# First feed-forward product of a Griffin-style block: 20 of 22 pairs by seven block products

## The chip, the cores and the metric

The kernel runs on one core of one Trainium2 chip. The metric is the device time of one execution in microseconds (us); the kernel before takes 917.13 us, the median of three runs (917.04 to 917.58).

The core has five engines that run side by side and wait for each other through semaphores: PE multiplies matrices, DVE (VectorE) and ACT (ScalarE) work on whole tiles, POOL (GpSimd) does slower tile work and can issue transfers, SP only issues transfers. Weight loads into PE have a row of their own, PEld. The profile's times count from the start of the span, which is the stretch from the first to the last instruction.

## What is computed

One layer of a streaming encoder over 512 tokens of 1024 features, all in float32: three parallel mixers, cross-attention into 256 memory tokens, and a gated feed-forward block. The change touches the last part only:

```python
h = rms_norm(x, g_ffn_pre[l])
f_gate, f_up = jnp.split(h @ w_ffn_in[l], 2, axis=-1)      # 1024 -> 2 x 2816
x = x + rms_norm((jax.nn.silu(f_gate) * f_up) @ w_ffn_out[l], g_ffn_post[l])
```

`w_ffn_in` is 1024 x 5632 and `w_ffn_out` 2816 x 1024.

## The kernel before

**Three matmuls for one.** Each float32 operand is kept as a high part, rounded to the matmul's own format by a cast on ACT, and a low part, the difference, made by a subtraction on DVE or POOL. A product is the sum of three matmuls, high by high, high by low and low by high (`mm3`, L89 to L92). So every weight tile costs a load on SP's queue (L173), a cast on ACT (L191) and a subtraction, either one on DVE (L195) or two halves on POOL (L198, L199). The list `low` says which engine is next; `low_on("g")` sends all to POOL, `low_on("v")` all to DVE, `low_on("vg")` alternates.

**First product, pair by pair.** 128 gate columns of `w_ffn_in` and the 128 up columns that belong to them are a pair; there are 22 pairs. A unit is one of the two: `unit` runs 8 chunks of 128 features, each `mm3` over all 512 tokens, 24 matmuls of 512 columns. A pair is two units, 48 matmuls. `hh` and `hl` hold the normed tokens turned to features, 8 chunks by 512 tokens. `swiglu` takes the two sums from PSUM: tanh on ACT (L1126), two DVE steps (L1127, L1128), and then the split of the result into high and low (L1129 on ACT, L1130 on DVE).

**The first two pairs** (`NFIRST` = 4 units) start before all tokens are normed: `unit_piece` does them in two halves of 256 columns, tokens 0 to 255 first. In between, token blocks 2 and 3 are normed and turned (`R[2].turn()`, `R[3].turn()`): `turn_pe` transposes on PE (L294), `turn_out` casts to `hh` on ACT (L302) and subtracts to `hl` on DVE (L303).

**Second product.** `project` runs over the 22 chunks of 128 hidden columns; each needs one tile of `w_ffn_out` and 24 matmuls of 512 columns over 4 token blocks.

**What sets the order.** Storage is taken from pools of slots, first given back, first taken: 6 raw weight tiles (RAW), 4 split ones (WH, WL), 8 PSUM banks (PS), 10 tiles of 128 x 512 (T2), 13 of 128 x 2048 by then (K8). The code is written in one sequence; a scheduler then sets the order on each engine, and each engine works strictly in it. `prefetch` splits weights two units ahead.

## Time and profile before

| | |
|---|---|
| median of three runs | 917.13 us |
| the profiled execution | 914.67 us |
| its span, first to last instruction | 912.9 us |
| granted clock of PE, mean | 0.997 of full speed |
| first two pairs, start of their matmuls | 537.67 us |
| the other 20 pairs | 563.3 to 783.7 us |
| second product and the end | 783.7 to 912.9 us |

The stages are read from the timeline of PE: the matmuls of the first product carry the names `hh,k` and `hh,x` with 256 columns (first two pairs) and `hh,wh` with 512 (the other pairs); those of the second have `wh` as the moving operand and `k` or `x` as the stationary one. A row of the timeline gives start, duration, engine, line and tiles; matmuls overlap, so the time that one takes out of PE is the distance between starts, not the duration. The profiled execution is 2.46 us shorter than the median; sums are made against the profiled one.

### The profile page before, as it was taken

How to read it: one execution, taken by the hardware profiler on the slowest of the kernel's cores; microseconds unless marked ns; L12 is line 12 of the kernel's file. 1: busy time of each engine (PE TensorE's matmuls, PEld its weight loads, DVE VectorE, ACT ScalarE, POOL GpSimd, SP SyncE). 2: the span in 40 equal slices, each digit the busy share in tenths (PEclk: the TensorE clock that was granted, in tenths of full speed). 3: DMA queues.
4: the chain of work that ended last, by engine and by line, in shares of the span. 5: the costliest groups of instructions: out<-in, count | busy, mean ns of one | idle time of the engine just before them, and what ended most of it. 6: DMA issues, size and time to landing. Idle time of an engine off the chain costs nothing.

```text
span 912.9 us, 11068 instructions
## 1 busy us (share of the span) xinstructions
PE 885.9 (97%) x4179; PEld 730.5 (80%) x4179; DVE 499.8 (55%) x889; ACT 344.3 (38%) x575; POOL 231.2 (25%) x203
## 2 busy tenths in 40 slices
PE   7999999999999999999989989999999999999997
PEld 6788888888788788888868779888888888888885
DVE  5769989946773745311876783433334443222225
ACT  4465553225654544322655452222223222211121
POOL 2223464644444322344561460000000000000000
PEclk9999999999999999999999999999999999999999
DMA  8953237333332245333454230333333332333102
GB/s 245 242 128 93 70 93 184 93 94 91 104 81 77 75 150 185 96 107 97 117 161 115 70 116 1 93 93 98 104 97 93 93 93 92 96 99 104 48 1 93
DMA packets 122801, 95.42 MB, mean 105 GB/s; under 512 B 5568, under 2 KB 111612, under 8 KB 122748
## 3 DMA queue, kind: packets, MB, share of 16 engines
q1 hardware_dynamic: 120172, 90.52, 34.5%
q10 hardware_dynamic: 2576, 4.19, 1.3%
q8 instruction: 33, 0.54, 0.2%
q14 instruction: 20, 0.16, 0.1%
HBM read 86.83 MB, written 2.10 MB: 97 GB/s over the span
## 4 chain that ended last, share of the span: by engine, by line
PE 88%; DVE 5%; issue 2%; ACT 2%; POOL 1%; DMA 1%; ACTq 0%; DVEq 0%; SPq 0%; POOLq 0%
PE ps L91 28%; PE ps L90 28%; PE ps L92 28%; PE ps L450 1%; PE ps L775 1%; PE ps L760 1%; PE ps L294 1%; DVE wl L195 1%; DVE hl L303 1%; DVE k L932 1%; POOL wl L199 1%; POOL y L274 1%; DVE c L278 0%; DVE k L393 0%; DMA k<-t 0%
## 5 line engine op out<-in xcount | busy, mean ns | idle before, releaser
L191 ACT CAST wh<-raw 128x1024 fp32r<-128x1024 f32 (+1 forms) x144 | 150.5, 1047 | 388.9 <-issue 154.3
L91 PE MATMUL ps<-hl,wh 128*128 128x512 f32 (+2 forms) x736 | 285.5, 388 | 3.7 <-DVE hl L303 3.7
L90 PE MATMUL ps<-hh,wh 128*128 128x512 f32 (+2 forms) x736 | 285.9, 389 | 0.3 <-ACT hh L302 0.3
L92 PE MATMUL ps<-hh,wl 128*128 128x512 f32 (+2 forms) x736 | 285.4, 388 | 0.0
L195 DVE TENSOR_TENSOR wl<-raw,wh 128x1024 fp32r<-128x1024 f32 x79 | 98.2, 1243 | 163.0 <-ACT wh L191 163.0
L91 PEld LDWEIGHTS ps<-hl,wh 128*128 128x128 f32 (+1 forms) x736 | 137.6, 187 | 34.0 <-DVE hl L303 4.6
L90 PEld LDWEIGHTS ps<-hh,wh 128*128 128x128 f32 (+1 forms) x736 | 137.4, 187 | 30.0 <-ACT hh L302 0.5
L92 PEld LDWEIGHTS ps<-hh,wl 128*128 128x128 f32 (+1 forms) x736 | 137.5, 187 | 29.7
L198 POOL TENSOR_TENSOR wl<-raw,wh 128x512 fp32r<-128x512 f32 (+1 forms) x65 | 88.9, 1368 | 199.4 <-ACT wh L191 178.2
L274 POOL TENSOR_TENSOR y<-u,half 128x1 f32<-128x1 f32 x26 | 15.1, 587 | 415.5 <-DVE u L271 384.6
L199 POOL TENSOR_TENSOR wl<-raw,wh 128x512 fp32r<-128x512 f32 (+1 forms) x65 | 91.8, 1412 | 0.0
L90 PE MATMUL ps<-wh,k 128*128 128x512 f32 x192 | 75.8, 395 | 0.0
L91 PE MATMUL ps<-wl,k 128*128 128x512 f32 x192 | 75.5, 393 | 0.0
L92 PE MATMUL ps<-wh,k 128*128 128x512 f32 x176 | 69.7, 396 | 0.0
L90 PE MATMUL ps<-k,wh 128*128 128x512 f32 (+1 forms) x128 | 47.2, 369 | 0.0
L1128 DVE TENSOR_TENSOR t<-t,ps 128x512 f32<-128x512 f32 x22 | 15.1, 688 | 58.5 <-PE ps L92 58.5
L92 PE MATMUL ps<-k,wl 128*128 128x512 f32 (+1 forms) x128 | 46.9, 366 | 0.0
L92 PE MATMUL ps<-wh,x 128*128 128x512 f32 x112 | 44.2, 395 | 0.0
L91 PEld LDWEIGHTS ps<-wl,k 128*128 128x128 f32 x192 | 36.1, 188 | 8.1
L90 PEld LDWEIGHTS ps<-wh,k 128*128 128x128 f32 x192 | 36.0, 188 | 8.2
L92 PEld LDWEIGHTS ps<-wh,k 128*128 128x128 f32 x176 | 33.4, 190 | 8.1 <-DVE k L393 0.2
L90 PE MATMUL ps<-wh,x 128*128 128x512 f32 x96 | 38.8, 404 | 0.0
(210 smaller groups left out, 1173.7 us busy)
## 6 DMA issues: line engine op xcount, KB each, us to landing
raw<-in_w_in SPq DMA_DIRECT2D x45, 512.0 KB, 4.0
raw<-in_w_ffn_in SPq DMA_DIRECT2D x44, 512.0 KB, 3.8
raw<-in_w_ffn_out SPq DMA_DIRECT2D x22, 512.0 KB, 3.5
raw<-in_w_branch SPq DMA_DIRECT2D x12, 512.0 KB, 3.4
k<-t SPq DMA_DIRECT2D x32, 128.0 KB, 2.4
raw<-in_w_out SPq DMA_DIRECT2D x8, 512.0 KB, 3.6
raw<-in_w_mem_kv SPq DMA_DIRECT2D x8, 512.0 KB, 3.6
k<-in_x ACTq DMA_DIRECT2D x2, 1024.0 KB, 8.9
```

The source lines that it names most:

```text
L90: T.matmul(o, lh, rh, start=start, stop=False, skip_group_check=True)
L91: T.matmul(o, lh, rl, start=False, stop=False, skip_group_check=True)
L92: T.matmul(o, ll, rh, start=False, stop=stop, skip_group_check=True)
L191: copy = A.copy(h, src)
L195: V.tensor_sub(l, src, f32(h))
L198: G.tensor_sub(l[:, :c], src[:, :c], f32(h[:, :c]))
L199: G.tensor_sub(l[:, c:], src[:, c:], f32(h[:, c:]))
L274: G.tensor_tensor(y, u, half, op=OP.pow)
L294: T.transpose(ps[:, k], src[:, (4 * q + k) * P:(4 * q + k + 1) * P], ident)
L303: V.tensor_sub(hl[:, 4 * q:4 * q + 4, dst], ps, f32(h))
L450: T.matmul(ps[:, :n], q[j][:, hp, r], k[i][:, :n], start=i == 0, stop=i == 1, skip_group_check=True)
L1128: V.tensor_mul(th, th, pu)
```

## The change

A pair is seen as a 2 x 2 matrix of blocks: gate and up columns by the first and the last 512 features (a11, a12 for gate, a21, a22 for up), and the tokens as 2 x 2 too (features 0 to 511 and 512 to 1023, by tokens 0 to 255, LO, and 256 to 511, HI: b11, b21, b12, b22). The 2 x 2 product of blocks is formed from seven block products in place of eight (Winograd's form of Strassen's scheme, with its signs placed otherwise). A block product is 4 chunks of `mm3` over 256 columns, 12 matmuls; a pair has 84 matmuls of 256 columns. The first two pairs and the second product keep their matmuls.

- **Weight sums** s1 to s4 per pair, each 128 x 512: s1 and s2 by additions on DVE, s3 and s4 by transfers that POOL issues and that add to their target (`accum_op`). `first`, `second` and `third` split two blocks each (cast 128 x 1024 on ACT, subtraction on DVE), `fourth` splits s4.
- **Token sums** t1 to t4, once: taken from the turned blocks while they are in PSUM. Blocks 0 and 1 are also copied whole to SBUF (`whole`), blocks 2 and 3 give differences (`turn_tokens`), and `token_sums` splits the four sums.
- **`swiglu`** writes the result unsplit; the split (`halve`) moves to the second product, up to 4 chunks ahead. `before` and `behind` are the hooks in `project`.
- **Order**: the sums and splits of the next pair are written between the products of this one; products 3 and 4 of a pair stand between the first products of the next one. The splits of the first four units are written ahead of the output projection of the memory attention (`prefetch(4 + NFIRST)`), and alternate between DVE and POOL; the two `low_on` settings in the first product are gone, so the tiles of `w_ffn_out` alternate too.

```diff
-        while (state["split"] < min(len(specs), want) and raws
+        while (state["split"] < min(state["last"], want) and raws
...
+    prefetch(4 + NFIRST)
...
     def after_o(t, pss):
         R.append(Residual(t, pss, g_post, g_next))
-        if t == 0:
-            low_on("g")
-            prefetch(4 + NFIRST)
...
+    whole = K8.take([P, 2, 4, 256])
+
+    def turn_tokens(t, pss):
+        if t < 2:
+            for q in range(2):
+                A.copy(whole[:, q, :, t * P:(t + 1) * P], pss[q])
+            PS.give(*pss)
+            return None
+        c12, d1, d3 = (T2.take([P, 4, P]) for _ in range(3))
+        A.copy(c12, pss[0])
+        V.tensor_sub(d1, whole[:, 0, :, (t - 2) * P:(t - 1) * P], pss[0])
+        V.tensor_sub(d3, pss[1], c12)
+        PS.give(*pss)
+        return c12, d1, d3
...
     def swiglu(m, pg, pu):
-        act_tiles(m)
         th = T2.take([P, S])
         A.activation(th, pg, AF.Tanh, scale=0.5)
         V.scalar_tensor_tensor(th, th, 1.0, pg, op0=OP.add, op1=OP.mult)
-        V.tensor_mul(th, th, pu)
-        A.activation(ah[m], th, AF.Copy, scale=0.5)
-        V.scalar_tensor_tensor(al[m], th, 0.5, f32(ah[m]), op0=OP.mult, op1=OP.subtract)
+        V.scalar_tensor_tensor(act_tile(m), th, 0.5, pu, op0=OP.mult, op1=OP.mult)
...
+    def token_sums(t, c12, d1, d3):
+        r = slice((t - 2) * P, (t - 1) * P)
+        d2, d4 = T2.take([P, 4, P]), T2.take([P, 4, P])
+        V.scalar_tensor_tensor(d2, d3, -1.0, whole[:, 0, :, r], op0=OP.mult, op1=OP.subtract)
+        V.scalar_tensor_tensor(d4, d2, -1.0, whole[:, 1, :, r], op0=OP.mult, op1=OP.subtract)
+        for name, src in (("t2", d2), ("t1", d1), ("t3", d3), ("t4", d4)):
...
+            h, l = (x[:, :, r] for x in tokens[name][:2])
+            tc.keep_in_program_order(A.copy(h, src))
+            tc.keep_in_program_order(V.tensor_sub(l, src, f32(h)))
...
+        def two(self, names, src, pin):
+            h, l = WH.take([P, KD, P], F32R), WL.take([P, KD, P], F32R)
+            both = self.split(names, src, h, l, pin)
...
+        def sums(self, pin=False):
+            s2, s1 = self.s[:, 0:4], self.s[:, 4:8]
+            ins = [V.tensor_add(s1, self.u_[:, 0:4], self.u_[:, 4:8]),
+                   V.tensor_add(s2, s1, self.g_[:, 0:4])]
...
+            G.dma_start(self.u_[:, 0:4], self.g_[:, 0:4], accum_op=OP.add)
+        def first(self, pin=False):
+            self.two(["a11", "a12"], self.g_, pin)
+        def second(self, pin=False):
+            self.two(["s2", "s1"], self.s, pin)
+        def third(self, pin=False):
+            self.two(["s3", "a22"], self.u_, pin)
+            RAW.give(self.u_)
+        def fourth(self, pin=False):
+            s4 = self.g_[:, 4:8]
+            G.dma_start(s4, self.s[:, 0:4], accum_op=OP.add)
+            h, l = T2.take([P, 4, P], F32R), T2.take([P, 4, P], F32R)
+            self.split([], s4, h, l, pin)
+            self.u["s4"] = (h, l, None)
+            RAW.give(self.g_)
+            load_ahead()
+        def product(self, o, a_, b, start, stop):
+            (h, l, both), (bh, bl) = self.u.pop(a_), tokens[b][:2]
+            for k in range(4):
+                mm3(o, h[:, k], l[:, k], bh[:, k], bl[:, k], start and k == 0, stop and k == 3)
...
+        def p1(self):
+            self.x, self.y = PS.take([P, 2, TH]), PS.take([P, S])
+            self.v, self.up = T2.take([P, S]), T2.take([P, S])
+            self.product(self.x[:, 0], "a11", "b11", True, False)
+            A.copy(self.v[:, LO], self.x[:, 0])
...
+        def p5(self):
+            self.product(self.y[:, HI], "s1", "t1", True, False)
+            V.tensor_add(self.up[:, HI], self.v[:, HI], self.y[:, HI])
+        def p7(self):
+            self.product(self.x[:, 1], "s3", "t3", True, False)
+            V.tensor_add(self.up[:, HI], self.up[:, HI], self.x[:, 1])
+        def p3(self):
+            self.product(self.y[:, HI], "s4", "b22", False, True)
+        def p4(self):
+            self.product(self.x[:, 1], "a22", "t4", False, True)
+            V.tensor_add(self.up[:, LO], self.v[:, HI], self.x[:, 1])
+            V.tensor_add(self.v, self.v, self.y)
...
-    for m in range(NFIRST // 2, NFF):
-        if m == NFIRST // 2 + 1:
-            low_on("v")
-        w0, w1 = take_w(), take_w()
-        pg, pu = PS.take([P, S]), PS.take([P, S])
-        unit(pg, w0)
-        unit(pu, w1)
-        swiglu(m, pg, pu)
+    while cur is not None:
+        nxt = Pair(cur.m + 1) if cur.m + 1 < NFF else None
+        if nxt is None:
+            state["last"] = len(specs)
+        cur.p1()
+        if nxt:
+            nxt.sums()
+        if old:
+            old.p3()
+        cur.p2()
+        if old:
+            old.p4()
+        if nxt:
+            nxt.first()
+        cur.p6()
+        if nxt:
+            nxt.second()
+        cur.p5()
+        cur.p7()
+        if nxt:
+            nxt.third()
+            nxt.fourth()
+        old, cur = cur, nxt
```

The scheduler's order moves at two places that matter here. The first is DVE in the pairs. Before, five rows make one pair: `wl` is the low part of a unit's weights, `ps` the two sums of a pair, `k` its result.

```order
L195 TENSOR_TENSOR wl_87_5220<-raw_91_4680,wh_87_5219 128x1024
L1127 SCALAR_TENSOR_TENSOR t_4_173_5213<-t_4_173_5213,ps_251_5163 128x512
L1128 TENSOR_TENSOR t_4_173_5213<-t_4_173_5213,ps_252_5164 128x512
L195 TENSOR_TENSOR wl_88_5226<-raw_92_4686,wh_88_5225 128x1024
L1130 SCALAR_TENSOR_TENSOR k_4_65_5134<-t_4_173_5213,k_8_64_5133 128x512
```

Now, the twelve rows of one pair's time. The matmuls of pair 6 (`ps_259`, `ps_260`) run meanwhile; `wl_98` to `wl_100` and `t_5_208` are the splits of pair 7 (`first`, `second`, `third`, `fourth`); L1206 and L1207 are the sums s1 of pair 9 and s2 of pair 9; L1259 and L1263 follow products 5 and 7 of pair 6, L1270 and L1271 product 4 of pair 5, L1275 and L1276 its result.

```order
L1192 TENSOR_TENSOR wl_98_5721<-raw_97_5409,wh_98_5720 128x1024
L1270 TENSOR_TENSOR t_8_200_5538<-t_1_199_5537,ps_257_5535 128x256
L1192 TENSOR_TENSOR wl_99_5738<-k_9_69_5067,wh_99_5737 128x1024
L1271 TENSOR_TENSOR t_1_199_5537<-t_1_199_5537,ps_258_5536 128x512
L1206 TENSOR_TENSOR k_9_69_5067<-raw_102_5656 128x512
L1259 TENSOR_TENSOR t_4_205_5661<-t_9_204_5660,ps_260_5659 128x256
L1192 TENSOR_TENSOR wl_100_5768<-raw_98_5411,wh_100_5767 128x1024
L1275 SCALAR_TENSOR_TENSOR t_6_206_5716<-t_6_206_5716,t_1_199_5537 128x512
L1263 TENSOR_TENSOR t_4_205_5661<-t_4_205_5661,ps_259_5658 128x256
L1276 SCALAR_TENSOR_TENSOR x_1_71_5596<-t_6_206_5716,t_8_200_5538 128x512
L1192 TENSOR_TENSOR t_5_208_5773<-raw_97_5409,t_3_207_5772 128x512
L1207 TENSOR_TENSOR k_9_69_5067<-k_9_69_5067,raw_101_5654 128x512
```

Five rows for a pair have become twelve, and two of the twelve (L1259, L1263) stand between a block product and a later product into the same part of a PSUM bank.

The second place is POOL where the memory attention ends and the first product begins. Before (`raw_87` to `raw_90` are the weights of pairs 2 and 3; L274 is a power of one column in the norms):

```order
L198 TENSOR_TENSOR k_9_60_4682<-raw_86_4439,k_9_60_4682 128x512
L199 TENSOR_TENSOR k_9_60_4682<-raw_86_4439,k_9_60_4682 128x512
L274 TENSOR_TENSOR y<-u,half 128x1 x5
L198 TENSOR_TENSOR wl_83_4893<-raw_87_4582,wh_83_4892 128x512
L199 TENSOR_TENSOR wl_83_4893<-raw_87_4582,wh_83_4892 128x512
L198 TENSOR_TENSOR wl_84_4900<-raw_88_4589,wh_84_4899 128x512
L199 TENSOR_TENSOR wl_84_4900<-raw_88_4589,wh_84_4899 128x512
```

Now:

```order
L198 TENSOR_TENSOR k_4_58_4605<-raw_86_4439,k_4_58_4605 128x512
L199 TENSOR_TENSOR k_4_58_4605<-raw_86_4439,k_4_58_4605 128x512
L274 TENSOR_TENSOR y<-u,half 128x1 x8
L1211 DMA raw_88_4587<-raw_87_4580 128x512
L1225 DMA raw_87_4580<-k_9_69_5067 128x512
L1211 DMA raw_90_4598<-raw_89_4592 128x512
L1211 DMA raw_92_4609<-raw_91_4603 128x512
```

The eight half-subtractions of pairs 2 and 3 (four of them stand in what is shown) are gone from POOL, and it goes on with the adding transfers, two for each pair.

More of the change, by code (lines that the diff above doesn't have):

```diff
@@ L166, in hybrid_block_kernel @@
     raws, ready = collections.deque(), collections.deque()
-    state = {"load": 0, "split": 0, "taken": 0, "low": 0}
+    state = {"load": 0, "split": 0, "taken": 0, "low": 0, "last": first_ffn + NFIRST}
     def load_ahead(n=None):
@@ L887, in project @@
             give_w(w)
+            if behind:
+                behind(k)
+        if before:
+            before(nk)
         ws = [take_w() for _ in range(hold)]
@@ L1139, in hybrid_block_kernel @@
             if c == 0 and i == 2:
-                R[2].turn()
                 R[3].norm()
+                ds = R[2].turn(turn_tokens)
         if c == 0:
-            R[3].turn()
+            token_sums(3, *R[3].turn(turn_tokens))
+            token_sums(2, *ds)
+            K8.give(whole)
+            tokens.update(b11=quad(0, 0), b21=quad(1, 0), b22=quad(1, 1))
+            scratch = K8.take([P, 2, KD, P])
+            cur = Pair(NFIRST // 2)
+            for f in (cur.first, cur.sums, cur.second, cur.third, cur.fourth):
+                f()
     give_w(*ws)
-    low_on("g")
     for m in range(NFIRST // 2):
```

104 lines of the change are left out of this document (86 added, 18 removed).

## The prediction

> **What bounds the kernel now.** I read the page first, then the table by stage, then the timeline of PE for what one matmul takes out of it.
>
> The page's busy times, and its chain that ended last by engine:
>
> ```profile
> span 912.9 us, 11068 instructions
> PE 885.9 (97%) x4179; PEld 730.5 (80%) x4179; DVE 499.8 (55%) x889; ACT 344.3 (38%) x575; POOL 231.2 (25%) x203
> ...
> PE 88%; DVE 5%; issue 2%; ACT 2%; POOL 1%; DMA 1%; ACTq 0%; DVEq 0%; SPq 0%; POOLq 0%
> ```
>
> PE is busy nearly throughout, and the chain is mostly PE. What the change is worth must be read in the stages it touches. The table by stage gives for each stretch its length, then busy time and count of PE, PEld, DVE, ACT and POOL, the granted clock, the share of DMA and GB/s:
>
> ```profile
> 563.30:783.70 220.40, 220.40 (x960) 179.92 (x959) 85.63 (x99) 61.59 (x79) 0.00 (x0) 1.00 0.32 93
> 783.70:912.90 129.20, 122.41 (x529) 98.96 (x528) 37.91 (x53) 25.96 (x36) 2.19 (x4) 0.99 0.21 70
> ```
>
> The first row is the 20 pairs: 960 matmuls, PE busy for the whole of 220.40 us at full clock, so 220.40 / 960 = 0.2296 us for one of 512 columns, and 48 x 0.2296 = **11.02 us for a pair**. DVE has 85.63 / 20 = 4.28 us of work in it, ACT 3.08, POOL none. Only fewer PE columns make this stage shorter.
>
> **The block products.** A matmul of 256 columns runs already, in the first two pairs; the timeline has its starts:
>
> ```profile
> 538.13 0.28 PE L92 MATMUL ps<-hh,k 128*128 128x256 f32 x1
> 540.65 0.28 PE L92 MATMUL ps<-hh,k 128*128 128x256 f32 x1
> 540.77 0.28 PE L90 MATMUL ps<-hh,x 128*128 128x256 f32 x1
> 546.28 0.28 PE L92 MATMUL ps<-hh,x 128*128 128x256 f32 x1
> 552.42 0.28 PE L91 MATMUL ps<-hl,k 128*128 128x256 f32 x1
> 563.21 0.28 PE L92 MATMUL ps<-hh,k 128*128 128x256 f32 x1
> ```
>
> From row to row the first two are 21 matmuls apart, the next two 47, the last two 91: 2.52 / 21 = 0.1200, 5.51 / 47 = 0.1172, 10.79 / 91 = 0.1186 us, half of 0.2296 and a little. A pair of 84 takes 84 x 0.1186 = 9.96 us (9.84 to 10.08), 1.06 less than 11.02. Twenty pairs: **21.2 us saved** (18.8 to 23.6), 199.2 in place of 220.4. One block product of 12 takes 1.42. This holds if all else that a pair needs fits into 9.96.
>
> **DVE and ACT in a pair.** The groups between 600 and 780 us, then two from other stretches (the last number before the second bar is ns of one):
>
> ```profile
> L195 DVE TENSOR_TENSOR wl<-raw,wh 128x1024 fp32r<-128x1024 f32 x33 | 40.4, 1225 | 66.0 <-ACT wh L191 66.0
> L1128 DVE TENSOR_TENSOR t<-t,ps 128x512 f32<-128x512 f32 x16 | 11.0, 688 | 44.9 <-PE ps L92 44.9
> L191 ACT CAST wh<-raw 128x1024 fp32r<-128x1024 f32 x33 | 34.7, 1052 | 130.5 <-issue 130.5
> L1126 ACT ACTIVATE t<-ps 128x512 f32<-128x512 f32 x17 | 10.1, 591 | 0.0
> L1129 ACT ACTIVATE k<-t 128x512 fp32r<-128x512 f32 x12 | 7.5, 626 | 0.0
> ```
>
> ```profile
> L393 DVE TENSOR_TENSOR vv<-ps,vv 128x256 fp32r<-128x256 f32 x1 | 0.4, 417 | 0.0
> L1024 ACT ACTIVATE t<-ps,mx 128x256 f32<-128x256 f32 x16 | 7.4, 477 | 3.9 <-DVE mx L1021 3.9
> ```
>
> The twelve DVE rows of a pair are three subtractions of 1024 columns, six operations of 512 and three of 256: 3 x 1.225 + 6 x 0.69 + 3 x 0.417 = 9.07 us by durations. By starts it is less, since one ends under the next:
>
> ```profile
> 641.57 1.23 DVE L195 TENSOR_TENSOR wl<-raw,wh 128x1024 fp32r<-128x1024 f32 x1 [0.49 <-ACT wh L191]
> 642.71 0.69 DVE L1130 SCALAR_TENSOR_TENSOR k<-t,k 128x512 fp32r<-128x512 f32 x1
> ```
>
> The step from one start to the next is 1.14 where the duration is 1.23. If each row overlaps its follower by that 0.09, it is 9.07 - 12 x 0.09 = 8.0. So DVE goes from 4.28 to between 8.0 and 9.07 in 9.96: it fits, with 0.9 to 2 us to spare, and is no longer an idle engine. ACT has 3 x 1.052 + 0.626 + 0.591 + 2 x 0.477 = 5.33, which fits easily.
>
> Order matters as much as the sum. PE runs, from product 1's start, products 1, 3 (of the pair before), 2, 4 (before), 6, 5, 7. The split slots of `first` of the next pair come free when product 2 ends, at 3 x 1.42 = 4.27; the cast follows (1.05) and the subtraction (1.23), to 6.5, or 6.9 with the column sums that may be ahead. Behind it in DVE's queue stand L1270, the 1024 of `second`, L1271, one s1, and then L1259 after product 5: 0.42 + 1.23 + 0.69 + 0.69 + 0.42 = 3.45, so until about 10.35. Product 3 adds into the place that L1259 reads, and starts at 9.96 + 1.42 = 11.38. Slack 1.0 us. L1263 before product 4 has 1.5 in the same way. I charge nothing for the waits, because PE's own products cover them; with the cover gone each microsecond over the slack costs 20 us in the loop.
>
> **The adding transfers.** Two of 256 KB for each pair, on POOL's queue. No transfer of the trace adds to its target. The nearest rows, with the median from issue to landing last:
>
> ```profile
> raw<-in_w_ffn_in SPq DMA_DIRECT2D x44, 512.0 KB, 3.8
> ...
> k<-t SPq DMA_DIRECT2D x32, 128.0 KB, 2.4
> k<-in_x ACTq DMA_DIRECT2D x2, 1024.0 KB, 8.9
> ```
>
> Bounds 2.4 to 8.9 us. I take 4.5: an adding transfer reads source and target, 512 KB in all like the load at 3.8, and POOL has to issue it (0.7 is my choice). A gain from them is excluded, since nothing of the kind is there now. What L, the time of one, is worth: s4 waits for the subtraction of `first` (it writes what that reads), its cast and subtraction stand in ACT's and DVE's queues, and `first` of the next pair stands behind them on both. Once round is 1.23 (subtraction) + L + 0.63 (cast of s4) + 0.48 (a copy of product 1, next on ACT) + 1.05 (cast) = L + 3.4. It paces the pairs when L is over 9.96 - 3.4 = **6.6 us**, and makes them slower than before over 11.02 - 3.4 = **7.6 us**. With 4.5 the cost is nothing; cover 2.1.
>
> The Trainium skill, "DMA: Bandwidth & Descriptors", section "Anatomy of one DMA — SWDGE (gpsimd) path", gives a fit of about 2.0 us plus bytes over 436e3 for a transfer that POOL issues; an estimate from it is 2.6 us for 256 KB, near the lower bound, and the sum would not change. No run here shows such a transfer.
>
> Raw weights stay longer: the gate tile of a pair is given back only after s4 is split, so its slot is loaded for three pairs on. With six slots and 3.8 us for a load, about one pair's time is left over; no cost. SP has nothing else to do there.
>
> **The hand-over into the first pairs.** Here POOL's subtractions go and DVE gets more. Before, POOL's halves stretch DVE's norms:
>
> ```profile
> 523.23 0.35 DVE L278 SCALAR_TENSOR_TENSOR c<-y,w 128x1 f32<-128x1 f32 x2 [0.61 <-POOL y L274]
> 523.50 0.28 DVE L279 SCALAR_TENSOR_TENSOR y<-c,y 128x1 f32<-128x1 f32 x2
> 523.70 1.28 DVE L932 SCALAR_TENSOR_TENSOR k<-k,y,gb 128x1024 f32<-128x1024 f32 x1
> 528.86 1.40 DVE L278 SCALAR_TENSOR_TENSOR c<-y,w 128x1 f32<-128x1 f32 x2 [0.61 <-POOL y L274]
> 530.19 1.31 DVE L279 SCALAR_TENSOR_TENSOR y<-c,y 128x1 f32<-128x1 f32 x2
> 531.42 2.37 DVE L932 SCALAR_TENSOR_TENSOR k<-k,y,gb 128x1024 f32<-128x1024 f32 x1
> ...
> 531.44 1.27 POOL L198 TENSOR_TENSOR wl<-raw,wh 128x512 fp32r<-128x512 f32 x1
> 532.66 2.26 POOL L199 TENSOR_TENSOR wl<-raw,wh 128x512 fp32r<-128x512 f32 x1
> ```
>
> ```profile
> 533.94 1.38 PE L294 MATMUL ps<-ident,k 128*128 128x128 f32 x8 [2.81 <-DVE k L932]
> ```
>
> The three norm steps took 523.23 to 524.98, 1.75 us, in one norm and 528.86 to 533.79, 4.93, in the other, where POOL subtracts; PE waited 2.81 for that one. Without those halves (the last POOL rows are adding transfers) it should take 1.75, and the wait of 2.81 goes.
>
> The Trainium skill, "SBUF — State Buffer", section "Who interferes with whom", says that a DVE instruction with two SBUF inputs and a GpSimd instruction that reads SBUF lock each other out for a whole instruction; 1.28 becoming 2.37 agrees. The same page of the Trainium skill, section "SBUF: two separate sides", warns that DVE operations in a two-port mode keep POOL from writing descriptors; an estimate of that here is one DVE instruction more for each adding transfer, 1.23, within the cover of 2.1, and no run here shows it.
>
> Against it: between the last norm and the low part of block 3, which the second halves of the first two pairs need, DVE now has a weight sum s1 and s2, two differences of block 2 and the subtraction of `second` in front, 4 x 0.69 + 1.23 = 4.0 us, beside block 2's own two. PE has, meanwhile, the rest of the first halves and the matmuls that need high parts only. From the last block's low part on, six steps of 0.69, one of 1.23 and five token subtractions stand before product 6 needs t2: 11 x 0.69 + 1.23 = 8.8, against 96 x 0.1186 + 2 x 1.42 = 14.2 us of PE, the second halves and products 1 and 2: hidden. I take a **gain of 1.5 us** for the place, from bounds of 2.81 gained and 4.0 lost, nearer the gain since products 1 and 2 of the first pair can fill part of the wait.
>
> **Second product.** The split is now there: for one k ACT 0.626, DVE 0.69, and half of the weight splits of `w_ffn_out` on DVE as before, the other half on POOL. One k is 24 x 0.2296 = 5.5 us of PE, while the row of 129.20 us has DVE at 37.91 and ACT at 25.96; 22 x 0.69 = 15.2 and 22 x 0.63 = 13.9 more fit, written up to four k ahead. Cost nothing; if the first split were not ahead, about 1.3 once. In the pairs it takes one cast and no DVE step away, both already counted.
>
> **Sum.** 914.67 - 21.2 - 1.5 = 892.0 for a profiled execution, whose like was 2.46 under the median: **894.5**, said as 895 against 917.13. This kernel's runs can't tell a change below 0.2%, 1.8 us, from none.
>
> **Rivals.**
>
> *DVE paces the pairs.* The adding transfers or POOL's part in them may stretch DVE's two-input steps as the halves did, 1.28 to 2.37, 1.1 more. Two such in a pair make 8.0 to 9.07 into 10.2 to 11.2, say 10.6 for the pace: saved 0.42 x 20 = 8.4, so 914.67 - 8.4 - 1.5 + 2.46 = **907**. For it: DVE's margin of 0.9 to 2. Against it: POOL does no arithmetic there.
>
> *The adding transfers pace the pairs, slower than before.* With L at the upper bound, 8.9, the ring is 12.3 us: 20 x 1.28 = 25.6 lost, 914.67 + 25.6 - 1.5 + 2.46 = **941**. It decides from L of 6.6, and is slower from 7.6. For it: adding is a form of transfer that no row shows, two of a pair stand behind each other on one queue, and 256 KB lands beside loads. Against it: the four-fold bytes are needed to reach 8.9 among plain rows.
>
> *The hand-over costs.* The 4.0 us of DVE in front of block 3's low part lie on the path and the 2.81 wait comes back through them: 914.67 - 21.2 + 4.0 + 2.46 = **900**, or with a late token sum some 902.
>
> *Half the columns are not half the time.* If the weight loads no longer hide (PEld has 179.92 / 959 = 0.188 us for one), a pair is 84 x 0.188 = 15.8 us, 95 us lost, 1012. The spacing of 0.1186 under the same three matmuls speaks against it; weights changed there with every matmul too.
>
> **Chances.** Forecast 0.62; DVE paces 0.14; hand-over 0.10; transfers pace 0.12, of which 0.02 end between 6.6 and 7.6; half columns 0.02. Faster is the forecast, DVE, the hand-over and that 0.02, less 0.03 for a DVE case that goes all the way to 11: 0.85. Within 0.2% 0.03, slower 0.12. The forecast's own range is 891 to 898 (917.13 - 23.6 - 2.81, and 917.13 - 18.8 with nothing gained at the hand-over); the range with the cases is **890 to 908**, which leaves out the transfers' case and half columns.
>
> **What would show it.** In the profile after: the spacing of the 256-column matmuls in the pairs at 0.117 to 0.120, a pair every 9.96, and hardly any idle time of PE with L1259, L1263 or a split as releaser; DVE near 8 to 9 us of work a pair, its 1024-column step still 1.23 and not 2.3; the adding transfers landing in under 6.6; no wait of 2.81 before the last turn, and less than 3 us of idle PE before the second halves of the first pairs; the second product within a microsecond of 129.2. I am wrong if PE waits in every pair: for DVE with busy steps, DVE paces; for a cast of s3 or s4 that waits on a transfer, the transfers do. Idle time once, before the first block product, is the hand-over.

## The result, and the profile after

| | before | after |
|---|---|---|
| median | 917.09 us (916.12 to 917.58) | 896.53 us (895.92 to 897.55) |
| ratio to before | | 0.9778, 95% interval 0.9761 to 0.9795 |
| profiled execution | 914.67 us | 897.55 us |
| its span | 912.9 us | 895.8 us |
| granted clock of PE, mean | 0.997 | 0.992 |
| first matmul of the first product | 537.67 us | 536.57 us |
| first matmul of the second product | 783.7 us | 766.53 us |
| second product and the end | 129.20 us | 129.27 us |

The forecast was 895 us, in a range of 890 to 908; the change saves 20.6 us. The two profiled executions differ by less, 17.1 us, since that of before is 2.4 us under its median and that of the change 1.0 over. Timed once more beside the experiments it had a median of 896.39 us and the same ratio, 0.9778 (0.9762 to 0.9794).

The page's busy times of the changed kernel, and its chain that ended last by engine:

```profile
span 895.8 us, 12981 instructions
PE 867.0 (97%) x4899; PEld 751.4 (84%) x4899; DVE 594.7 (66%) x1059; ACT 399.7 (45%) x669; POOL 283.6 (32%) x255
...
PE 82%; DVE 9%; issue 3%; DMA 2%; POOL 2%; ACT 2%; ACTq 0%; DVEq 0%; SPq 0%; POOLq 0%
```

PE is still the busy engine. The chain leans less on it, and on DVE more: some waits have come in. The table by stage of the changed kernel, in a long stretch of steady pairs, in the stretch ahead of it, and in the second product:

```profile
566.00:590.00 24.00, 21.98 (x173) 21.77 (x173) 16.84 (x25) 9.56 (x14) 5.26 (x6) 0.93 0.76 165
590.00:760.00 170.00, 170.00 (x1441) 170.00 (x1440) 139.38 (x205) 87.48 (x123) 28.63 (x33) 1.00 0.70 156
766.53:895.80 129.27, 122.69 (x530) 98.95 (x528) 46.05 (x62) 32.42 (x48) 30.41 (x24) 0.98 0.24 74
```

In the middle row PE never waits: 170 / 1441 = 0.1180 us for a matmul, 84 x 0.1180 = **9.91 us for a pair** where it was 11.02. DVE works 139.38 / 170 of that time, 8.1 us a pair, ACT 5.1. The first row is another matter: 2 us idle and a clock of 0.93, with the DMA engines busy three quarters of the time. One pair's time of the steady stretch, on DVE, ACT, POOL and PE (the timeline: start, duration, engine, line, tiles; in brackets the wait ahead of a row and what ended it):

```profile
638.84 1.23 DVE L1192 TENSOR_TENSOR wl<-raw,wh 128x1024 fp32r<-128x1024 f32 x1 [1.75 <-ACT wh L1192]
...
642.05 0.69 DVE L1206 TENSOR_TENSOR k<-raw 128x512 f32<-128x512 f32 x1
642.65 0.41 DVE L1259 TENSOR_TENSOR t<-t,ps 128x256 f32<-128x256 f32 x1
...
648.82 1.23 DVE L1192 TENSOR_TENSOR wl<-raw,wh 128x1024 fp32r<-128x1024 f32 x1 [1.75 <-ACT wh L1192]
```

```profile
643.82 0.63 ACT L1192 CAST t<-raw 128x512 fp32r<-128x512 f32 x1 [0.22 <-DMA raw<-k]
...
647.74 1.05 ACT L1192 CAST wh<-raw 128x1024 fp32r<-128x1024 f32 x1 [2.42 <-PE ps L91]
```

```profile
640.47 0.90 POOL L1225 DMA_DIRECT2D raw<-k  x1 [6.40 <-DVE t L1270]
```

```profile
644.75 0.28 PE L90 MATMUL ps<-hh,t 128*128 128x256 f32 x1
```

The adding transfer for s4 is issued at 640.47, and the cast that needs it starts at 643.82: 3.35 us. Behind that cast ACT waits 2.42 us for PE before the next `first`, so the transfers have room. L1259, which the next matmul into its place needs at 644.75 (`hh,t` is product 3), is done at 643.06: 1.7 us of slack.

**Where the time goes.** The account is made on the two profiles, 912.9 and 895.8 us. From the first matmul of the first product to the first of the second it was 246.03 us and is 229.96: 16.1 less. The steady pace alone is worth 20 x (11.02 - 9.91) = 22.2, so 6.1 are missing. The list of PE's waits, by what ended them (total, times, longest), shows most of them:

```profile
PE ps L90 <- DVE t L1259: 2.9, 2, 2.0
...
PE ps L90 <- DVE t L1114: 0.9, 1, 0.9
```

L1259 is waited for once in the fourth pair, 2.02 us, and once in the last, 0.87. What leads to the first of these, from the timelines of POOL, ACT, DVE and PE of the changed kernel, in this order:

```profile
567.36 1.78 POOL L1211 DMA_DIRECT2D raw<-raw  x2 [15.54 <-DVE k L1206]
```

```profile
572.51 1.05 ACT L1192 CAST wh<-raw 128x1024 fp32r<-128x1024 f32 x1 [3.16 <-DMA raw<-raw]
```

```profile
573.59 1.23 DVE L1192 TENSOR_TENSOR wl<-raw,wh 128x1024 fp32r<-128x1024 f32 x1 [2.65 <-ACT wh L1192]
...
582.56 0.69 DVE L1206 TENSOR_TENSOR k<-raw 128x512 f32<-128x512 f32 x1 [2.32 <-DMA raw<-in_w_ffn_in]
583.17 0.41 DVE L1259 TENSOR_TENSOR t<-t,ps 128x256 f32<-128x256 f32 x1
```

```profile
583.64 0.39 PE L90 MATMUL ps<-hh,t 128*128 128x256 f32 x1 [2.02 <-DVE t L1259]
```

And the table by stage for the 4 us behind it (its third number from the right is the granted clock):

```profile
584.00:588.00 4.00, 4.00 (x24) 4.00 (x23) 3.46 (x6) 0.56 (x2) 0.55 (x1) 0.59 0.76 150
```

Read from the top: the first sums of pair 3 are late, since the splits of the token sums stand ahead of them on DVE (558.57 to 563.46); so POOL issues the adding transfers of pair 3 only from 567.36 on, `third` of pair 3 splits only at 573.59 and s4 at 575.75, and only behind these two are its raw slots loaded again, at 574.85 and 576.47 (issues on SP). The two loads are for pair 6. Its sum s1 (L1206) reads the second of the tiles and waits for it until 582.56, with L1259 of pair 3 in the queue behind. Nobody needs s1 of pair 6 for two more pairs; PE needs L1259 at once, and waits. Then, in the last row, the clock is 0.59 for 4 us: another 4 x 0.41 = 1.6 us. With the waits (2.02 + 0.87 + 0.85 at L1114 + 0.2 for L303 + 0.17 for L302, less 0.24 that was there before) that makes 5.5 of the missing 6.1; the rest I do not place.

Ahead of the first product the two profiles differ by 1.1 us, and this is not like with like: in the 4 us from 472 us, a stage that no edit touches, the clock is 1.00 in the one and 0.57 in the other (both rows stand in the last section), which is 1.7 us. Two of the runs below pair up better, when the time is counted from the matmul at which PE resumes there. The run with the later s1 has the code of the change up to its first product, and full clock at 472 us. It resumes at 471.40, and its first product starts here:

```profile
534.31 0.28 PE L90 MATMUL ps<-hh,k 128*128 128x256 f32 x1
```

That is 62.91 us, against 66.49 in the kernel before (471.18 to 537.67): 3.6 less. The run with half columns has the code of before up to this point, and clocks of 0.90 and 0.68 in the 8 us from 468. It takes 68.02 us (471.53 to 539.55), against 64.45 in the change (472.12 to 536.57): 3.6 again. So the hand-over gains 3.6 us, of which the two profiles of the table show 1.1.

The wait of 2.81 is gone: the three norm steps ahead of the turn that had it take 1.74 us (532.21 to 533.95) in place of 4.93, and the turn follows without idle time. Gone with it is the low clock behind it (0.82 and 0.76 in the 8 us from 532 in the profile of before, 1.7 us). A new wait has come in the memory attention, on DVE, where POOL subtracts at the same time, and on PE:

```profile
507.38 2.15 DVE L195 TENSOR_TENSOR k<-raw,k 128x1024 fp32r<-128x1024 f32 x1
509.45 1.23 DVE L1030 TENSOR_SCALAR mx<-mx 128x4 f32<-128x4 f32 x1
```

```profile
511.33 0.50 PE L91 MATMUL ps<-k,k 128*128 128x512 f32 x1 [1.52 <-DVE k L394]
...
534.30 1.03 PE L294 MATMUL ps<-ident,k 128*128 128x128 f32 x8
```

The low part of an early split takes 2.15 in place of 1.22 and holds up what stands behind it: a step of the softmax (L1030), and then the low part (L394) that PE waits for. Of the 1.52, 0.67 was there before, at another row; 2.81 + 1.7 less the new 0.85 is 3.7, about what the four profiles say.

### The profile page after: what moved, and what is told of

It is laid out like the page before. It is cut to its first block, busy times and chain, and to the rows that moved or that the text cites. A ratio compares the mean times of both kernels' runs of the same rounds, so it can differ in the third digit from the quotient of the medians.

```text
span 895.8 us, 12981 instructions
## 1 busy us (share of the span) xinstructions
PE 867.0 (97%) x4899; PEld 751.4 (84%) x4899; DVE 594.7 (66%) x1059; ACT 399.7 (45%) x669; POOL 283.6 (32%) x255
## 4 chain that ended last, share of the span: by engine, by line
PE 82%; DVE 9%; issue 3%; DMA 2%; POOL 2%; ACT 2%; ACTq 0%; DVEq 0%; SPq 0%; POOLq 0%
PE ps L91 26%; PE ps L92 26%; PE ps L90 26%; PE ps L451 2%; DVE hl L303 1%; PE ps L776 1%; POOL y L274 1%; DVE k L394 1%; DMA raw<-k 1%; DMA raw<-in_w_ffn_in 1%; PE ps L761 1%; DVE wl L195 1%; POOL wl L199 1%; DVE k L939 0%; DVE c L278 0%
## 5 line engine op out<-in xcount | busy, mean ns | idle before, releaser
L191 ACT CAST wh<-raw 128x1024 fp32r<-128x1024 f32 (+1 forms) x104 | 108.5, 1046 | 227.8 <-PE ps L91 111.7
L91 PE MATMUL ps<-hl,wh 128*128 128x512 f32 (+2 forms) x576 | 206.7, 359 | 3.3 <-DVE hl L303 3.3
L90 PE MATMUL ps<-hh,wh 128*128 128x512 f32 (+2 forms) x576 | 207.1, 360 | 1.2 <-DVE t L1114 0.9
L92 PE MATMUL ps<-hh,wl 128*128 128x512 f32 (+2 forms) x576 | 206.3, 358 | 0.0
L91 PEld LDWEIGHTS ps<-hl,wh 128*128 128x128 f32 (+1 forms) x576 | 108.9, 189 | 20.2 <-DVE hl L303 4.3
L90 PE MATMUL ps<-k,wh 128*128 128x256 f32 (+1 forms) x368 | 114.6, 311 | 0.0
L92 PE MATMUL ps<-k,wl 128*128 128x256 f32 (+1 forms) x368 | 114.2, 310 | 0.0
L91 PE MATMUL ps<-k,wh 128*128 128x256 f32 (+1 forms) x336 | 105.3, 313 | 0.0
L92 PEld LDWEIGHTS ps<-k,wl 128*128 128x128 f32 x368 | 69.4, 188 | 4.3
L90 PEld LDWEIGHTS ps<-k,wh 128*128 128x128 f32 x368 | 69.4, 189 | 4.1
L1192 ACT CAST wh<-raw 128x1024 fp32r<-128x1024 f32 x40 | 42.0, 1051 | 61.2 <-PE ps L91 53.1
L91 PEld LDWEIGHTS ps<-k,wh 128*128 128x128 f32 x336 | 63.3, 188 | 4.2
```

Of the source, the lines that this page charges most:

```text
L90: T.matmul(o, lh, rh, start=start, stop=False, skip_group_check=True)
L91: T.matmul(o, lh, rl, start=False, stop=False, skip_group_check=True)
L92: T.matmul(o, ll, rh, start=False, stop=stop, skip_group_check=True)
L191: copy = A.copy(h, src)
L1192: ins = [A.copy(h, src), V.tensor_sub(l, src, f32(h))]
```

## The experiments

Every median is beside runs of the kernel before on the same chip (916.6 to 916.9 us); ratios are to it. Where "the change" is compared, its ratio is 0.9778 (0.9761 to 0.9795).

| run | median | ratio, 95% interval |
|---|---|---|
| hand-over alone, on the kernel before | 916.0 | 0.9991 (0.9982 to 1.0000) |
| half columns, on the kernel before | 924.47 | 1.0086 (1.0067 to 1.0104) |
| s1 later | 891.68 | 0.9733 (0.9717 to 0.9748) |
| s3 and s4 on DVE | 893.42 | 0.9747 (0.9734 to 0.9760) |
| two transfers for s4 | 925.65 | 1.0084 (1.0056 to 1.0112) |
| three transfers for s4 | 936.93 and 951.46, one execution each | |
| four more DVE operations a pair | 930.4 | 1.0140 (1.0117 to 1.0162) |
| s1 later and two more waits out | 893.17 | 0.9738 (0.9714 to 0.9761) |
| s1 later and the wait at the end out | 892.68 | 0.9732 (0.9710 to 0.9755) |
| s1 later, old hand-over | 894.82 | 0.9758 (0.9735 to 0.9781) |
| the change again | 896.39 | 0.9778 (0.9762 to 0.9794) |

### Half columns: is 0.118 us the price of 256 columns?

```diff
-        unit(pg, w0)
-        unit(pu, w1)
+        for o, w in ((pg, w0), (pu, w1)):
+            for c in range(2):
+                unit_piece(o, w, c * 256, c * 256 + 256)
+            give_w(w)
```

> The kernel before, with each unit of the 20 pairs done in two halves of 256 columns: 96 matmuls of 256 in place of 48 of 512, with the same arithmetic and nothing else changed. My theory: a matmul of 256 columns takes 0.118 us wherever it stands, so a pair takes 11.33 in place of 11.02 us, 6.1 us more over 20 pairs: 923. Rival (the weight load, 0.188 us, shows when the columns are halved): 96 x 0.188 = 18 us for a pair, about 140 us more. Rival (half is exactly half): no change.

924.47 us, 7.6 more than before. The table by stage of this run:

```profile
590.00:760.00 170.00, 170.00 (x1430) 170.00 (x1429) 63.75 (x75) 46.63 (x60) 0.00 (x0) 1.00 0.32 94
```

170 / 1430 = 0.1189 us, without a wait, and 96 x 0.1189 = 11.41 for a pair. So the main term of the forecast stands by itself: halves cost 3 to 4% more than half, weight loads stay hidden, and seven eighths of 96 matmuls is where the gain comes from.

### The later s1: is the late load the cause of the wait?

```diff
-            V.tensor_add(self.up[:, HI], self.up[:, HI], self.x[:, 1])
+            self.last = V.tensor_add(self.up[:, HI], self.up[:, HI], self.x[:, 1])
...
-        if nxt:
+        if nxt and len(done) > 1:
+            with tc.issue_after(done[-2].ins):
+                nxt.sums()
+        elif nxt:
             nxt.sums()
...
+        done.append(cur.last)
```

> The changed kernel, with the sum s1 of the pair three ahead queued on DVE behind the step that follows product 7, in place of ahead of the step that follows product 5. My theory: the wait of 2.02 us of PE in the fourth pair is a late load of raw weights that s1 waits for, with the step after product 5 queued behind it; with s1 behind, the wait goes, and with it the stretch of granted clock 0.59 that follows it, 1.6 us: 3.7 us faster than the change, 892.9. If the low clock has nothing to do with the wait: 2.0 faster. Rival (the load is late for whatever comes next, so the wait moves to another step): no difference, 896.5.

891.68 us; the two intervals against the change do not meet. The table by stage for the stretch that held the wait:

```profile
566.00:590.00 24.00, 24.00 (x206) 24.00 (x205) 20.00 (x30) 12.78 (x18) 5.25 (x6) 1.00 0.77 167
```

PE is busy throughout, at full clock; before the edit it was 21.98 of 24 at 0.93. The rival, that the wait moves on, falls. From the first matmul of the first product to the first of the second it is 226.11 us (534.31 to 760.42) in place of 229.96, 3.85 less, close to the 3.7 that was expected.

### The change again: does the low clock belong to the wait?

No edit.

> The change itself once more, timed in five rounds like the runs it is compared with. My theory (the wait of 2.02 us for the late load and the stretch of low granted clock behind it belong to this kernel, not to one execution): 896.5, both in the profile again, and 4 to 5 us slower than the run with the later s1. Rival (the low clock behind that wait was chance): the wait is there, the clock is full, and the time is nearer 894.5.

896.39 us. The profile has the wait and not the low clock. PE's timeline in this run, and the 4 us behind the wait in its table by stage:

```profile
582.10 0.39 PE L90 MATMUL ps<-hh,t 128*128 128x256 f32 x1 [1.73 <-DVE t L1259]
```

```profile
584.00:588.00 4.00, 4.00 (x37) 4.00 (x35) 3.67 (x7) 2.10 (x2) 0.12 (x1) 1.00 1.10 253
```

So the wait is the kernel's own, and the low clock behind it was not there in this execution, which took 894.48 us, where the rival put it; the median, 896.39, is where the theory put it. Its stretch from first to second product is 228.12 us (535.34 to 763.46): 2.0 over the run with the later s1, the wait and 0.3. The medians are still 4.7 us apart. For the executions without a profile the record has the mean granted clock: 0.992 to 0.995, 0.993 in the mean, in the five of this run, and 0.994 to 0.998, 0.995 in the mean, in the five with the later s1. The difference of 0.002 over 895 us is an estimate of 1.8 us, which with the 2.0 makes 3.8 of the 4.7. Where in those executions the clock was low, and that the wait was the reason, is not shown.

### s3 and s4 on DVE: are the transfers needed?

```diff
-            G.dma_start(self.u_[:, 0:4], self.g_[:, 0:4], accum_op=OP.add)
+            V.tensor_add(self.u_[:, 0:4], self.u_[:, 0:4], self.g_[:, 0:4])
...
-            G.dma_start(s4, self.s[:, 0:4], accum_op=OP.add)
+            V.tensor_add(s4, s4, self.s[:, 0:4])
```

> The changed kernel, with s3 and s4 added on DVE in place of by adding transfers. DVE's work in a pair goes from the measured 8.1 us of 9.9 to 9.3 by starts (two more of 0.6), or to 10.5 by durations (9.07 + 1.38). My theory (what counts is the distance between starts): it still fits into 9.91, the pairs keep their pace, and the time is that of the change within 2 us, or up to 3 us less, since the first pairs no longer wait for transfers. Rival (DVE paces, or its order makes PE wait): 0.6 us for each pair, 908 or so.

893.42 us, 3 less than the change. The table by stage:

```profile
590.00:740.00 150.00, 150.00 (x1271) 150.00 (x1271) 144.24 (x215) 74.56 (x106) 0.00 (x0) 1.00 0.37 106
```

DVE is busy 144.24 of 150, 9.5 us a pair, and PE never waits. The sum by starts was right, the one by durations was not: at 10.5 a pair could not take 9.9. From first to second product it is 226.10 us (536.14 to 762.24), to 0.01 that of the run with the later s1. So the adding transfers gain nothing in this kernel; they take DVE's load from 96% to 82%, and nothing else asks for that time. Without them the DMA engines are busy 0.37 in place of 0.70, and no load is late.

### Four more DVE operations: from where does DVE pace?

```diff
-            ins = [V.tensor_add(s1, self.u_[:, 0:4], self.u_[:, 4:8]),
-                   V.tensor_add(s2, s1, self.g_[:, 0:4])]
+            ins = [V.tensor_add(s1, self.u_[:, 0:4], self.u_[:, 4:8]) for _ in range(3)]
+            ins += [V.tensor_add(s2, s1, self.g_[:, 0:4]) for _ in range(3)]
```

> The changed kernel, with each of s1 and s2 computed three times into the same place: four more DVE operations of 512 columns for a pair, results unchanged. DVE's work goes from 8.1 to 10.5 us for a pair of 9.91. My theory (DVE paces once its starts fill the time of the products): 0.6 us for a pair, 12 us slower than the change, 909. Rival (the order decides, not the sum: the steps after products 5 and 7 come too late well before DVE is full): 25 us or more. Rival (DVE is never waited for): 896.5.

930.4 us, 34 more than the change: the middle one of the three, the order, and my theory is wrong by nearly three times. Three rows of its table by stage, and two of its list of PE's waits:

```profile
590.00:640.00 50.00, 47.10 (x382) 45.60 (x383) 45.98 (x71) 21.31 (x31) 6.99 (x8) 1.00 0.60 140
640.00:690.00 50.00, 44.66 (x357) 42.77 (x357) 45.43 (x69) 19.97 (x29) 7.90 (x9) 1.00 0.61 141
690.00:740.00 50.00, 45.16 (x361) 43.19 (x361) 44.91 (x70) 20.56 (x30) 7.90 (x9) 1.00 0.57 129
```

```profile
PE ps L92 <- DVE wl L1192: 12.5, 17, 0.8
PE ps L90 <- DVE t L1259: 5.9, 8, 1.4
```

1100 matmuls in 150 us are 11.45 us a pair, and DVE is busy 10.4 of them. It is not full, for it waits itself. From 590 to 740 us, DVE waits for ACT's cast of s4 (first row), and that cast for the adding transfer (second row):

```profile
DVE t L1192 <- ACT t L1192: 8.8, 11, 1.5
...
ACT t L1192 <- DMA raw<-k: 12.6, 13, 1.5
```

So the pairs are long although DVE is only 91% busy: PE waits for low parts that stand behind sums, and DVE for a cast that waits for a transfer. The run above has nearly as much work on DVE (9.5 in 9.9) and no wait, but it has no adding transfers either. How much of the 34 us is the order of the queue and how much the transfer inside it, these two runs do not separate.

### Two transfers for s4: the ring

```diff
-            G.dma_start(s4, self.s[:, 0:4], accum_op=OP.add)
+            G.dma_start(s4, self.s[:, 4:8], accum_op=OP.add)
+            G.dma_start(s4, self.g_[:, 0:4], accum_op=OP.add)
```

> The changed kernel, with s4 made by two adding transfers one behind the other (s1, then a11: the same sum) in place of one (s2). One takes 3.35 us from issue to the cast that waits for it, so the way from the end of the subtraction of first to the cast of s4 goes from the measured 3.75 to 7.1 us. My theory (the ring of the prediction, L + 3.4): 10.5 us for a pair in place of 9.91, 12 us slower than the change, 908. By the idle time that the trace shows on ACT behind the cast of s4, 2.42 us, it is 3.35 - 2.42 = 0.93 for a pair, 19 us slower, 915. Rival (the transfers are off every path): the time of the change, 896.5.

925.65 us, 29 more than the change. In this run, two issues on POOL, the casts of s4 that follow them on ACT (both from the timelines), and the table by stage:

```profile
639.84 0.88 POOL L1225 DMA_DIRECT2D raw<-k  x1 [5.12 <-DVE t L1271]
...
652.37 0.89 POOL L1225 DMA_DIRECT2D raw<-k  x1 [5.57 <-DVE t L1271]
```

```profile
648.88 0.62 ACT L1192 CAST t<-raw 128x512 fp32r<-128x512 f32 x1 [5.74 <-DMA raw<-raw]
...
659.56 0.62 ACT L1192 CAST t<-raw 128x512 fp32r<-128x512 f32 x1 [4.32 <-DMA raw<-raw]
```

```profile
590.00:640.00 50.00, 45.14 (x376) 44.32 (x376) 35.75 (x53) 22.44 (x33) 10.78 (x13) 1.00 0.83 165
640.00:690.00 50.00, 44.14 (x365) 43.23 (x365) 34.58 (x51) 21.27 (x31) 11.36 (x13) 1.00 0.80 161
690.00:740.00 50.00, 44.47 (x367) 43.45 (x367) 36.12 (x53) 19.39 (x28) 12.42 (x14) 1.00 0.79 155
```

From first issue to cast it is 9.04 and 7.19 us, 8.1 in the mean, not the 6.7 of two times 3.35: with five transfers a pair on the DMA engines each takes longer (median from issue to landing 4.0 for the first and 4.2 for the others on POOL's queue, where the change has 3.3 and 3.8). L + 3.4 with this L is 11.5; 1108 matmuls in 150 us are 11.4 a pair. The rest of the ring, from the cast of s4 to the next issue, is 3.49 us here (648.88 to 652.37), and 3.48 or 3.49 in each of the fourteen pairs from 593 to 755 us, while L goes from 7.1 to 9.2 in them. So the ring of the prediction is there and has the size it was given, and the slower-than-before rival would have come true at an L of 7.6. What was wrong in the expectation is that one more transfer costs what one costs alone.

A third transfer (`G.dma_start(s4, self.g_[:, 0:4], accum_op=OP.add)` once more) was to give the slope.

> As the run with two adding transfers for s4, with a third one (a11 is added twice, so s4 and the result are other values). If the transfers are a ring that paces the pairs once it is longer than the products, every further one costs its whole 3.35 us for each of 20 pairs: 67 us more than with two, 975 to 982. Rival: the slope is smaller, because the queue takes the next transfer before the one ahead has landed: less than 30 us more than with two.

In this execution the granted clock was 0.65 throughout, in the unchanged stages too (1217 us in all), so it says nothing of transfers. Again:

> The run with three adding transfers for s4 once more, since the granted clock was 0.65 in the whole of the first one, the stages ahead of the first product too. By the ring, L + 3.4: with two transfers L was 9.04 and 7.19 us in two neighbouring pairs, 8.1 in the mean, and a pair took 11.4. A third of 4.1 us makes L 12.2 and a pair 15.6: 84 us more than with two, 1010. If the clock falls in the pairs, because PE waits some 5 us in each: more than 1030. Rival (the slope is smaller): under 960.

936.93 and 951.46 us in two executions, with mean clocks of 0.986 and 0.972. The first is 11.3 us more than with two, on the rival's side, and it is a single execution. From the list of PE's waits in the other, which was profiled (total, times, longest):

```profile
PE ps L90 <- ACT t L1257: 36.3, 14, 5.2
```

PE waits in it for a copy on ACT (L1257, after product 6), 3.8 to 5.2 us in one of two pairs between 655 and 770 us, and no longer for DVE. The ring's formula asked for 84 us. It holds for the order in which every s4 stands between two `first`s on both queues; with a third transfer PE's waits come in every other pair, and I have no formula for that. It stays open.

### The hand-over, alone and put back

On the kernel before, with nothing else changed:

```diff
     mem_tr(2)
+    prefetch(4 + NFIRST)
+    low_on("v")
...
     def after_o(t, pss):
...
-        if t == 0:
-            low_on("g")
-            prefetch(4 + NFIRST)
```

> The kernel before, with only the hand-over changed: the splits of the first four units are written ahead of the output projection of the memory attention and alternate between DVE and POOL, and all later splits go to DVE. The first product and the second stay as they were. My theory (POOL's subtractions stretch the norms, and PE's wait of 2.81 us follows from it): the wait before the last turn goes, and with it a stretch of low granted clock behind it that the profile of before shows (0.82 and 0.76 in 8 us, about 1.7 us); about 0.9 us is given back in the memory attention, where a split now stands in the way. Together 3.6 us faster than before, 913.5. Rival (the wait only moves to another place): within 1 us of before.

916.0 us, within 0.2% of before: 3.6 was expected, and the rival holds. PE's timeline in this run, the rows with new waits:

```profile
511.59 0.50 PE L91 MATMUL ps<-k,k 128*128 128x512 f32 x1 [1.54 <-DVE k L393]
...
539.50 0.39 PE L91 MATMUL ps<-hl,k 128*128 128x256 f32 x1 [2.01 <-DVE hl L303]
...
552.69 1.06 PE L294 MATMUL ps<-ident,x 128*128 128x128 f32 x8 [1.20 <-DVE x L932]
```

The wait of 2.81 became three, of 1.54 (0.67 of it was there before, at another row), 2.01 and 1.20. Of the low parts of pairs 2 and 3, two tiles are now made on DVE (at 536.54, ahead of the L303 that PE waits 2.01 us for, and at 541.35), and four halves in place of eight on POOL, from 535.91 on, behind the norm that had the wait. So this edit is more than an earlier prefetch. The wait of 2.81 does go, as expected, and the first two pairs lose what that gains.

The other way round, on the kernel with the later s1:

```diff
-    prefetch(4 + NFIRST)
...
     def after_o(t, pss):
         R.append(Residual(t, pss, g_post, g_next))
+        if t == 0:
+            low_on("g")
+            prefetch(4 + NFIRST)
+            low_on("vg")
```

> The kernel of the run with the later s1, with the hand-over put back towards the kernel before: the splits of the first four units are written behind the first block of the output projection again, three of the four low parts on POOL. Theory of the prediction (the early prefetch is what keeps POOL off DVE's norms): the norms of the third and fourth block are stretched again and PE waits for one of them, 2 to 3 us slower than the run with the later s1, 894. Rival (what stretched the norms were the low parts of pairs 2 and 3, which the change no longer makes on POOL, and the early prefetch itself gives nothing or costs the 0.9 us it takes in the memory attention): 890.8 to 891.7.

894.82 us, 3.1 more than with the later s1. By the time alone the theory's 894 is nearer than the rival's 890.8 to 891.7; but the intervals of the two ratios overlap, and the early prefetch is worth between nothing and some 5 us. The traces speak for the rival: PE waits for no norm at the turns of the first two blocks, and the stretch from first to second product is 226.34 us (536.50 to 762.84) against 226.11. From the matmul at which PE resumes at 471.30 to its first product it takes 65.20 us, 2.3 more than the 62.91 above, and most of these, up to 1.7, are a low clock from 468 to 476 us (0.84 and 0.73), which the other profile does not have; some 0.6 to 0.9 are left. In the memory attention PE has another wait in place of the 1.52 (the list of its waits in this run):

```profile
PE ps L1048 <- DVE t L1038: 2.3, 3, 0.9
```

What took the 2.81 us away, then, is not that the first splits come earlier: the last of them on POOL, of `raw_86`, starts at 507.15 us in the change and at 507.17 in the kernel before. It is that no low part of pairs 2 and 3 stands on POOL beside the norms any more. That is a part of the block products, not of the prefetch. What the early prefetch is worth in the time stays open.

### Two more waits

```diff
...
-    prefetch(4 + NFIRST)
+    with tc.issue_after(scores_end[3].ins):
+        prefetch(4 + NFIRST)
...
-        halves(acts[k], t[:, 0], t[:, 1])
+        if k in (2, 3):
+            with tc.issue_after(done[-1].ins):
+                halves(acts[k], t[:, 0], t[:, 1])
+        else:
+            halves(acts[k], t[:, 0], t[:, 1])
```

Both edits, on top of the later s1 (`scores_end[3]` is the last step of the scores of the fourth head):

> The kernel of the run with the later s1, with two more waits taken out of the order: the splits of the first four units are queued on DVE behind the last step of the scores of the memory attention, so that PE no longer waits 1.5 us for a low part there (0.7 of it was there before the change), and two of the first splits of the second product are queued behind the step after product 7 of the last pair, so that PE no longer waits 0.87 us there. Expected 1.7 us faster than the run with the later s1, 890.0. Rival (the splits only push other work back, and the first pairs start later): the same 891.7 or slower.

893.17 us: no gain over the later s1 alone. The wait of 1.52 in the memory attention is gone, and one of 1.32 stands at the turn of the second block (PE's timeline in this run):

```profile
533.78 1.06 PE L294 MATMUL ps<-ident,k 128*128 128x128 f32 x8 [1.32 <-DVE k L939]
```

The second edit without the first:

> The kernel of the run with the later s1, and of the other two waits only the one at the end of the pairs taken out (two first splits of the second product behind the step after product 7 of the last pair); the splits ahead of the memory attention's output projection stay where the change has them. The wait of 0.87 us of PE goes, or shrinks to the 0.28 that the run with three waits taken out shows: 0.6 to 0.9 us faster than the run with the later s1, 890.9. Rival (the other end of the same chain is late then): 891.7.

892.68 us, not to be told from 891.68. In its trace the wait at the end of the pairs is gone, and the stretch from first to second product is 225.51 us (536.20 to 761.71), 0.6 less than with the later s1 alone, the least that the expectation gave; in the median 0.6 us does not show. The best kernels of the study are these with the later s1, which the times do not tell apart: 0.9733 and 0.9732 of the time before, about 4 us below the change (0.0045 of 917).

## Why the prediction was right

The time, 896.53 for 895, is 1.5 us off, and the mechanism was right: the steady pairs pay what the spacing of the matmuls says. That it is so near is in part luck, since the other terms were off in both directions: the main term was 1 us too small, the hand-over about 2 too small, and waits and low clock in the first and last pairs, which the prediction did not have, took 5.5 to 6 back.

- **The block products.** Said: 9.96 us a pair, 21.2 saved. Measured: 9.91 and 22.2 at the steady pace, and 0.1189 us a matmul in the run with half columns. This step carries the result.
- **DVE in a pair.** Said: between 8.0 and 9.07, 0.9 to 2 us to spare, slack 1.0 (L1259). Measured: 8.1, and 1.7 of slack. The lower bound, by starts, was the right one: the run with the sums on DVE holds 9.5 in 9.9. The rival's point, however, was put at a full DVE, and the run with four more operations shows 11.45 us a pair with DVE at 91%: its waits for the casts, and the order of its queue, bind before the sum does.
- **The adding transfers.** Said: 4.5 us in bounds of 2.4 to 8.9, hidden up to 6.6. Measured: 3.35 from issue to the cast that waits. The fit of the Trainium skill, "DMA: Bandwidth & Descriptors", section "Anatomy of one DMA — SWDGE (gpsimd) path", gave an estimate of 2.6; the medians from issue to landing on the page, the last number of the rows below, are 3.8 and 3.3, so adding, or the company of the loads, costs about 1 us over it. The ring was tested by a second transfer and held: its rest is 3.49 us where 3.4 was said.

```profile
raw<-in_w_ffn_in SPq DMA_DIRECT2D x44, 512.0 KB, 4.3
...
raw<-raw POOLq DMA_DIRECT2D x20, 256.0 KB, 3.8
raw<-k POOLq DMA_DIRECT2D x20, 256.0 KB, 3.3
```

- **Raw weights: the step that failed.** Said: "With six slots and 3.8 us for a load, about one pair's time is left over; no cost." That is so in steady pairs. In the first ones the token sums hold up the adding transfers, these the splits, and these the slots, and a load came late for s1 of a pair three ahead. It cost 2.02 and 1.73 us of waiting in the two profiles of the change; taking it out gains about 4 us in the time. I had looked at the hand-over for late low parts and late token sums, and at the ring for steady pairs; the transfers' start behind the token sums is where the two meet.
- **The hand-over.** Said: 1.5 gained, since POOL's halves no longer stretch a norm; its steps should take 1.75 and the wait of 2.81 should go. The reason held, and so did the figure: 1.74, and no wait. The size was too small: 3.6 between profiles that are alike. The low clock behind the wait went too, which the prediction left out; the wait of 1.52 in the memory attention, which it did not have either, is already taken off. My later expectations credited the early prefetch instead. Alone, on the kernel before, that edit gives 0.8 us, which is within 0.2%.
- **The second product.** Said: within a microsecond of 129.2. Measured 129.27, with DVE at 46.05 and ACT at 32.42. The place at which it costs is its seam with the last pair, 0.87 us, and there it was given nothing.

## What to carry to other kernels

A scheme with fewer matmuls pays what the steady pace says if the engines that make its sums have room in their order, and not only in their total; count the work by starts, and then ask what stands directly ahead of each step that PE waits for. Work that is needed far ahead (here a sum for a pair three ahead) belongs behind the steps that are needed now, since one late load at its head stops the whole queue. And when an edit is credited with a gain, run it alone: the early prefetch was, and gave 0.8 us of the 3.6 expected. Before two profiles are compared, look for low clock in the stages that no edit touches: here it hid about half of what the hand-over gains.

## What the runs showed of the hardware

PE's clock can be low behind waits that are quite short, and not each time. Behind the 2.81 us wait of the kernel before, 0.82 and 0.76 for 8 us; behind the 2.02 of the change 0.59 for 4 us; behind a wait of 1.73 at the same place in its other profile nothing. The same wait in a stage that no edit touches, 2.8 to 2.9 us at about 471 us, was followed by a clock of 1.00 in the kernel before and 0.57 in the change (the table by stage, before first):

```profile
472.00:476.00 4.00, 4.00 (x19) 3.23 (x18) 0.85 (x1) 0.24 (x1) 0.00 (x0) 1.00 1.08 320
```

```profile
472.00:476.00 4.00, 3.88 (x10) 3.12 (x11) 1.80 (x3) 0.00 (x0) 0.00 (x0) 0.57 0.84 262
```

Of the 13 profiles whose clock is not low throughout, 11 have it behind this wait; the kernel before and the run with the later s1 do not. Such a stretch is about 1.7 us that no instruction shows, and in some about twice that (0.81, 0.50 and 0.84 from 468 to 480 us with the hand-over alone). It comes and goes between executions of one kernel; this sets how small a difference can be told. The Trainium skill, "TensorE: Matmul & The Clock Gate", section "Part 1: The HAM clock gate", has the clock at one half or whole, and a fall after an idle window of about 3.4 us. A mean of 0.57 to 0.59 over 4 us agrees with 3.3 to 3.4 us at half clock. The threshold does not agree: here waits of 2.0 to 2.9 us were enough. Nor is the run with 0.65 throughout at one half or whole: stretches of 1 us of it have 0.65 too.

Transfers that add do not slow DVE: its 512-column operations take 0.684 us beside them, where POOL's subtractions stretch a 1024-column one from 1.22 to 2.15. Transfers slow each other once there are enough of them: from 590 to 740 us the raw loads land in 5.7 us (median) with three adding transfers a pair, and in 4.2 in the run with none (the sums on DVE). With two the effect is not shown: 4.3 in the change, but 3.9 with the later s1.
